# LayerNorm's sums back on VectorE, ties in the order of VectorE's work, and a buffer ring for the second FFN matrix, in a hybrid decoder block on one Trainium2 core

## The chip, the cores and the metric

The kernel runs on one core of a Trainium2 chip. The core has a matrix engine (TensorE, PE in the profile; its weight loads are a row of their own, PEld), a vector engine (VectorE, DVE), a scalar engine (ScalarE, ACT), a general engine (GpSimd, POOL) and a queue engine (SyncE, SP). DMAs are issued from the queues of SP, POOL and ACT. The metric is the device time of one execution in microseconds, as the median of several runs.

## The reference

One layer of a decoder trunk on a sequence of 1024 tokens with a width of 1024, in float32. A token-mixing sub-layer runs a convolution branch and an attention branch side by side and merges them by gates; a SwiGLU sub-layer follows. Cut to what matters:

```python
h = rmsnorm(x, pre_mix_g) * (1 + sc1) + sh1
proj = h @ w_in                                   # conv input, q, k, v, and two gates of 1024 columns
u = u_val * sigmoid(u_gate)
u = causal_depthwise_conv(u, conv_w, conv_b)      # 512 channels, 31 taps
u = silu(layernorm(u, conv_ln_g, conv_ln_b))      # over the 512 channels
y_conv = u @ w_conv_out
y_att = stick_breaking_attention(q, k, v) @ w_att_out
merged = sigmoid(g_conv) * y_conv + sigmoid(g_att) * y_att
x = x + ga1 * rmsnorm(merged @ w_o, post_mix_g)
h = rmsnorm(x, pre_ffn_g) * (1 + sc2) + sh2
gate, up = split(h @ w_ffn_in)                    # 2 x 2816 columns
x = x + ga2 * rmsnorm((silu(gate) * up) @ w_ffn_out, post_ffn_g)
```

`layernorm` takes, for each token, the mean over the 512 channels, subtracts it, and divides by the root of the mean square.

## The kernel before, in words

All activations are held transposed: channels on the 128 partitions, tokens along the free dimension, in two halves of 512 tokens. Float32 products are made from rounded parts: each operand is split into a rounded part ("hi", made by ScalarE) and the remainder ("lo", made by VectorE), and a product is three matmuls (hi hi, hi lo, lo hi) that accumulate in a bank of PSUM. So each operand costs a copy on ScalarE and a subtraction on VectorE.

The gate projections, the FFN's input product and its output product use Winograd's form of the 2 x 2 block product: seven block products instead of eight, for a few additions of weight blocks ("forms" s1 to s4) and of activation blocks (T1 to T4).

The stages in order of time are: the pre-norm and the conditioning vector; projections, convolution and attention; the gate products; the two branch projections and the merge; the product with w_o; the FFN's input product, block by block (`ffn(f)`, 22 blocks); the FFN's output product in four sweeps.

The change touches five places.

1. The gate products and LayerNorm (about 430 to 560 us). `other_five(i)` does, for each of eight pairs of weight tiles, five of the seven block products: T2 into bank ka, T1 into bank kc, T3 onto ka, B22 onto kc, T4 onto ka. Between them VectorE copies the banks out: v = ka + p1 (L814) after T2, w = kc + p1 (L816) after T1. T3 adds onto ka's bank, so it has to wait for v. The forms are s2 (L807), s3 (L809) and s4 (L811) on VectorE. `pair_load(i)` brings the weights (gw*a, gw*b), and s1 with a load and an accumulating DMA from POOL's queue (L795). Each finished piece goes through a sigmoid and out to DRAM from POOL's queue (`sig_out`).

   `ln_all` stands behind the third pair in the program. It loads the four channel tiles of the convolution's output (cr, 128 x 1024 each), and then, for each half of the tokens, makes the sum over the four tiles in `s0_` (the first half of the tile la): one plain load from SP and three accumulating DMAs from POOL (L854), each of which waits for the one before. A matmul with ones (lnm, L856) sums over the partitions. The mean is subtracted from the four tiles (L863), squares are made and added (L865, L867; `s0_` holds one of the squares in between), a second matmul with ones (lnv, L869) sums these, and the reciprocal root, which is put into `s0_` again, multiplies the four tiles (L873). So the second half's sum can enter `s0_` only when the first half has been multiplied.

2. `load_w` loads a tile of weights and splits it (rounding on ScalarE, remainder on VectorE, L153). Behind the merge (L954, L955: y times its gate, and added) the products with w_o begin, one `load_w` for each of eight column blocks.

3. The first blocks of the FFN's input product are written out by hand, in an order that is pinned on TensorE, VectorE and ScalarE. `ffn(0)` and `ffn(1)` are generators, and each `next(...)` emits the next piece of one; `t4(j)` makes T4's block j and its rounding, `lo_of` its remainder (L1228). The second `next(r1)` emits the splits of s2, and a later one those of s1 and s3.

4. `w2_forms(j)` prepares the forms of the FFN's second matrix for the last stage, one call behind each of the blocks f = 10 to 20. It loads four raw blocks (w2r), makes four forms in place (L1118, L1120, L1122, L1124), splits each (L1115) and stores it. Raw blocks come from the ring `wt` of nine buffers, out of which `ffn(f)` takes its s1, s2 and s3 (L1489, L1490, L1497) too. In the same rounds VectorE adds T3's result onto w (L1523), which frees ka's bank for T4.

Everything that isn't pinned is ordered by a planner, which goes through the instructions by priority (the order of the program, moved by offsets), with its own estimates of durations and landing times, and gives each engine and each DMA queue a fixed order. Each engine then runs its order strictly; waits are semaphores between the engines. A tie ("NoSync" dependency) only says in which order two instructions of one engine are to be put; it adds no semaphore.

Of the kernel before, what the change touches and what calls it, by code (L numbers as in the profile page):

```python
# [69 lines left out]
def tile_block(ctx: ExitStack, tc: tile.TileContext, xT, vecs, ada1, ada2, win, wv, wcv, wat, wo, w1, w2, cvw, out):  # L70
# [26 lines left out]
    def load(dst, src):  # L97
        return nc.sync.dma_start(dst, src)
# [648 lines left out]
    with ExitStack() as sG:  # L747
# [32 lines left out]
                load(b, xm_d[k][:, c * CH:(c + 1) * CH])  # L780
            t_ops(j, b11, b12, b21, b22, lambda name: ot(name, F32R))

        pairs, p1s, s1s, t3_done = {}, {}, {}, []

        def pair_load(i):
            wg = wp.tile([P, T], F32, tag="wraw", name=f"gw{i}a")
# [14 lines left out]
        def other_five(i):  # L801
            wg, wu = pairs[i]
            p1 = c21 = p1s[i]
            a11, a12, a21, a22 = wg[:, :CH], wg[:, CH:], wu[:, :CH], wu[:, CH:]
            s1, (s2, s3) = s1s[i], (st(f"g{nm}_{i}") for nm in ("s2", "s3"))
            v, w_ = xt(f"gv_{i}"), xt(f"gw_{i}")
            dve.tensor_tensor(s2, s1, a11, op=ALU.subtract)  # L807
            s2o = w_op(f"s2o_{i}", s2, act, GP)
            dve.tensor_tensor(s3, a11, a21, op=ALU.subtract)  # L809
            s4 = s2  # L810
            dve.tensor_tensor(s4, a12, s2, op=ALU.subtract)  # L811
            ka, kc = bkg(f"ka_{i}"), bkg(f"kc_{i}")
            prod0(ka, s2o, "T2")
            dve.tensor_tensor(v, ka, p1, op=ALU.add)  # L814
            prod0(kc, w_op(f"s1o_{i}", s1, act, GP), "T1")
            dve.tensor_tensor(w_, kc, p1, op=ALU.add)  # L816
            prod0(ka, w_op(f"s3o_{i}", s3, act, GP), "T3", False)
            t3_done.append(nc.cur_bb.bb.instructions[-1].name)
            dve.tensor_tensor(w_, ka, w_, op=ALU.add)
            sig_out(w_, 2 * i + 1, 1)  # L820
            prod0(kc, w_op(f"s4o_{i}", s4, act, dve), "B22", False)
            dve.tensor_tensor(v, kc, v, op=ALU.add)
            sig_out(v, 2 * i, 1)
            prod0(ka, w_op(f"a22_{i}", a22, act, dve), "T4", False)
            dve.tensor_tensor(c21, ka, p1, op=ALU.add)
            sig_out(c21, 2 * i + 1, 0)
# [17 lines left out]
        def ln_all():  # L844
            cr = [hp.tile([P, T], F32, tag="act", name=f"cr{ct}") for ct in range(CONVT)]
            for ct in range(CONVT):
                load(cr[ct], channels(u_d[ct]))
            la, lm = (hp.tile([P, 2, CH], F32, tag="act", name=f"l{nm}") for nm in "am")
            s0_, s1_, mean, sq = la[:, 0], la[:, 1], lm[:, 0], lm[:, 1]
            for c in range(NCH):  # L850
                cs = hs[c]
                load(s0_, channels(u_d[0])[:, cs])
                for ct in (1, 2, 3):
                    nc.gpsimd.dma_start(s0_, channels(u_d[ct])[:, cs], accum_op=ALU.add)  # L854
                pm = psg.tile([P, CH], F32, tag="ln", name=f"lnm{c}", bufs=1)
                mm_ = pe.matmul(pm, ones, s0_, start=True, stop=True)  # L856
                if c == 0:
                    tc.add_manual_dep(mm_.ins, t3_done[0], mybir.DependencyInfo(
                        mybir.DependencyClass.NoSync, mybir.DependencyReason.SCHED_ONLY))
                act.activation(mean, pm, AF.Copy, bias=0.0, scale=1.0 / 512)  # L860
                for ct in range(CONVT):
                    t = cr[ct][:, cs]
                    dve.tensor_tensor(t, t, mean, op=ALU.subtract)  # L863
                    q = (s1_, sq, s0_, sq)[ct]
                    act.activation(q, t, AF.Square)  # L865
                    if ct:
                        dve.tensor_tensor(s1_, s1_, q, op=ALU.add)  # L867
                pvv = psg.tile([P, CH], F32, tag="ln", name=f"lnv{c}", bufs=1)
                pe.matmul(pvv, ones, s1_, start=True, stop=True)  # L869
                rstd_from(s0_, mean, s1_, pvv, 512)  # L870
                for ct in range(CONVT):
                    t = cr[ct][:, cs]
                    dve.tensor_tensor(t, t, s0_, op=ALU.mult)  # L873
            for ct in range(CONVT):
                if ct < 2:
                    back = hp.tile([P, 2, CH], F32R, tag="act", name=f"cb{ct}")
                    back = [back[:, q] for q in range(2)]
                elif ct == 2:
                    back = [sgp.tile([P, CH], F32R, tag="sg", name=f"cb{ct}{q}", bufs=3) for q in range(2)]
                else:  # L880
                    back = pg.tile([P, 2, CH], F32R, tag="cb", name=f"cb{ct}", bufs=1)
                    back = [back[:, q] for q in range(2)]
                chi.append((hhi[HK + ct][:, :CH], back[0]))
                clo.append((hlo[HK + ct][:, :CH], back[1]))
                a, sg, o = cr[ct], flat(la), flat(lm)
                g, b_ = vec[:, C_LNG + ct:C_LNG + ct + 1], vec[:, C_LNB + ct:C_LNB + ct + 1]
                act.activation(sg, a, AF.Sigmoid, bias=b_, scale=g)
                act.activation(a, a, AF.Identity, bias=b_, scale=g)
                ar, sr = (t.rearrange("p (r m) -> p r m", r=PH) for t in (a, sg))
                dve.tensor_tensor(o.rearrange("p (m r) -> p r m", r=PH), ar, sr, op=ALU.mult)  # L890
                for c in range(NCH):
                    act.activation(chi[ct][c], o[:, hs[c]], AF.Copy)
                for c in range(NCH):
                    dve.tensor_tensor(clo[ct][c], o[:, hs[c]], chi[ct][c], op=ALU.subtract)
# [49 lines left out]
        for n in range(KT):  # L944
# [6 lines left out]
            for c in range(NCH):  # L951
                cs = slice(c * CH, (c + 1) * CH)
                load(sg[c], s_d[8 + n][:, cs])
                last = dve.tensor_tensor(sg[c], yb[c], sg[c], op=ALU.mult)  # L954
                dve.tensor_tensor(y[:, cs], y[:, cs], sg[c], op=ALU.add)  # L955
                if n < KT - 1:
                    continue
                if c == 0:
# [35 lines left out]
    with ExitStack() as sF:  # L994
# [80 lines left out]
        load(cb2, cb_d)  # L1075
        for n in range(KT):
            yb = dbank(f"pwo0_{n}")
            w = load_w(wo[n], f"wo0_{n}", act, dve)
            wo_part(yb, w, 0, 0, KT)
            pairs_w[n] = w  # L1080
            if n == HK:
                xr_load(0)
            if n < KT - 1:
                last = evac(0, n, yb)
                for col in ((), (32, 33), (34, 35), (36, 37), (38,), (39,), ())[n]:
                    w = flat2(y2(f"ada2_{col}"))
                    load(w, ada2[col - 2 * KT])
                    with tc.issue_after(last.ins):
                        dot_c(w, cb2, col)
# [15 lines left out]
                              stop=(j == HK - 1 and s == 2), skip_group_check=not first)  # L1105

        def w2_forms(j):
            a11, a12, a21, a22 = (wtmp(f"w2r{q}_{j}") for q in range(4))
            for q, t in enumerate((a11, a12, a21, a22)):
                load(t, w2[j][:, q])  # L1110

# [480 lines left out]
        next(r0)  # L1592
        for j in (2, 3):
            t4(j)
        next(r1)
        for j in (2, 3):
            lo_of("T4", j, h2[HK + j, 0])
        next(r1)
        next(r0)
        next(r0)  # L1600
# [383 lines left out]
```

## Time and profile before

| | us |
|---|---|
| median of 3 runs (lowest, highest) | 1392.19 (1386.76, 1393.64) |
| profiled execution, its own time | 1391.6 |
| its span, first to last instruction | 1389.8 |
| TensorE busy in it | 1370.6 (99%) |
| VectorE busy | 1041.0 (75%) |
| ScalarE busy | 658.5 (47%) |
| GpSimd busy | 122.9 (9%) |

The profile is one execution. "Busy" is the time in which an engine had an instruction running; TensorE's matmuls overlap, so that 512 columns take 0.39 us from start to end and start every 0.23 us. A line such as `L856` is the line of the kernel; where a helper issues the instruction, the line is the helper's, and the names of the tiles (out<-in) tell which call it was. In a list of waits the numbers are the total in us, how often, and the longest. In a timeline they are the start, the duration, the engine, the line, the operation, its tiles and shapes, how many are merged, and in brackets the idle time before and what ended it. In a table of windows each row is a stretch from the span's start, with its length, the busy time of an engine (and its instructions), the granted TensorE clock, the DMA engines' share and the GB/s moved.

### The profile page before, as it was taken

How to read it: one execution, taken by the hardware profiler on the slowest of the kernel's cores; microseconds unless marked ns; L12 is line 12 of the kernel's file. 1: busy time of each engine (PE TensorE's matmuls, PEld its weight loads, DVE VectorE, ACT ScalarE, POOL GpSimd, SP SyncE). 2: the span in 40 equal slices, each digit the busy share in tenths (PEclk: the TensorE clock that was granted, in tenths of full speed). 3: DMA queues.
4: the chain of work that ended last, by engine and by line, in shares of the span. 5: the costliest groups of instructions: out<-in, count | busy, mean ns of one | idle time of the engine just before them, and what ended most of it. 6: DMA issues, size and time to landing. Idle time of an engine off the chain costs nothing.

```text
span 1389.8 us, 18884 instructions
## 1 busy us (share of the span) xinstructions
PE 1370.6 (99%) x6832; PEld 1154.0 (83%) x6832; DVE 1041.0 (75%) x1593; ACT 658.5 (47%) x1169; POOL 122.9 (9%) x268
## 2 busy tenths in 40 slices
PE   8999999999999989999999999999999999999998
PEld 6898888998987868888887888888888888888887
DVE  7997786675877668887597987778787775884354
ACT  6565564464665446413366543324444443433442
POOL 0100001000001221000012200001111110000002
PEclk9999999999999999999999999999999999999999
DMA  9512051141569775865745545456767679596736
GB/s 379 229 41 66 16 167 46 46 137 46 182 222 363 221 209 201 297 222 173 297 137 189 197 144 180 139 194 246 251 224 263 248 257 383 182 346 209 253 114 122
DMA packets 98062, 272.38 MB, mean 196 GB/s; under 512 B 10416, under 2 KB 21808, under 8 KB 96944
## 3 DMA queue, kind: packets, MB, share of 16 engines
q1 hardware_dynamic: 75088, 204.30, 43.4%
q0 software_dynamic: 20160, 61.88, 13.6%
q10 hardware_dynamic: 2720, 4.98, 0.9%
q8 instruction: 54, 0.88, 0.3%
q14 instruction: 40, 0.33, 0.1%
HBM read 199.82 MB, written 71.30 MB: 195 GB/s over the span
## 4 chain that ended last, share of the span: by engine, by line
PE 85%; DMA 7%; DVE 4%; issue 1%; ACT 1%; SPq 0%; ACTq 0%; DVEq 0%; POOLq 0%
PE ka L1104 12%; PE ka L1651 8%; PE kc L1104 7%; PE pwo L1022 6%; PE ke L1213 4%; PE pb L1651 4%; PE pgv L164 3%; PE pya L164 3%; PE pyc L841 3%; PE pv L559 3%; PE ka L459 3%; PE k L459 3%; PE pgg L164 2%; PE pk L164 2%; PE pcv L538 2%; PE pq L164 2%
## 5 line engine op out<-in xcount | busy, mean ns | idle before, releaser
L633 ACT ACTIVATE ka<-z 128x128 f32<-128x128 f32 (+2 forms) x96 | 47.3, 495 | 45.5 <-PE z L632 33.8
L1651 PE MATMUL ka<-gt,w2f 128*128 128x512 f32 x264 | 63.4, 389 | 0.0
L639 DVE TENSOR_TENSOR_SCAN ka<-ka,eye 128x128 f32<-128x128 f32 (+1 forms) x64 | 51.3, 816 | 11.9 <-ACT ka L633 11.7
L644 DVE TENSOR_TENSOR be<-be,ka 128x127 f32<-128x127 f32 (+2 forms) x96 | 53.8, 573 | 6.9 <-ACT be L635 2.0
L1651 PEld LDWEIGHTS ka<-gt,w2f 128*128 128x128 f32 x264 | 49.6, 188 | 10.3
L119 DVE SCALAR_TENSOR_TENSOR ada<-ada,cb 128x1024 f32<-128x1024 f32 x32 | 39.0, 1224 | 18.1 <-DMA ada<-in_ada_dram 17.9
L635 ACT ACTIVATE be<-z 128x127 f32<-128x127 f32 (+2 forms) x96 | 46.9, 496 | 5.4 <-PE tr L658 5.2
L658 PE MATMUL tr<-ident,be 128*128 128x128 f32 x288 | 46.5, 272 | 0.3 <-DVE be L644 0.3
L1213 PE MATMUL ke<-b,w_hi 128*128 128x512 f32 x176 | 44.3, 394 | 0.0
L642 DVE TENSOR_TENSOR_SCAN ka<-ka 128x512 f32<-128x512 f32 x32 | 40.6, 1275 | 3.7 <-ACT ka L633 3.6
L538 PE MATMUL pcv<-ph,cvw 128*128 128x128 f32 x320 | 42.8, 275 | 0.0
L538 PEld LDWEIGHTS pcv<-ph,cvw 128*128 128x128 f32 x320 | 40.3, 191 | 1.0 <-DMA cvw<-in_cvw_dram 0.3
L664 ACT ACTIVATE ahi<-tr 128x512 fp32r<-128x512 f32 x48 | 28.2, 602 | 25.9 <-PE tr L658 17.8
L459 PE MATMUL k<-hhi,a 128*128 128x512 f32 x128 | 40.4, 391 | 0.0
L1213 PEld LDWEIGHTS ke<-b,w_hi 128*128 128x128 f32 x176 | 33.0, 188 | 7.7 <-issue 1.0
L143 ACT ACTIVATE gt<-X 128x512 fp32r<-128x512 f32 x33 | 20.3, 629 | 39.5 <-PE ka L1651 12.5
L665 DVE TENSOR_TENSOR alo<-tr,ahi 128x512 fp32r<-128x512 f32 x48 | 32.1, 685 | 7.8 <-ACT ahi L664 7.5
L658 PEld LDWEIGHTS tr<-ident,be 128*128 128x128 f32 x288 | 34.7, 140 | 3.6 <-PE z L632 0.6
L559 PE MATMUL pv<-wv_hi,hhi 128*128 128x256 f32 x128 | 36.8, 288 | 0.2 <-DVE klo L599 0.2
L559 PE MATMUL pv<-wv_hi,hlo 128*128 128x256 f32 x128 | 36.5, 285 | 0.0
L1637 DVE TENSOR_TENSOR gt<-X,gt 128x512 fp32r<-128x512 f32 x33 | 22.4, 690 | 18.8 <-ACT gt L143 18.7
L559 PE MATMUL pv<-wv_lo,hhi 128*128 128x256 f32 x128 | 36.2, 284 | 0.0
(550 smaller groups left out, 4169.1 us busy)
## 6 DMA issues: line engine op xcount, KB each, us to landing
w_d<-w2o POOLq DMA_DIRECT2D x44, 512.0 KB, 7.6
w2f<-w_d SPq DMA_DIRECT2D x44, 512.0 KB, 4.3
ada<-in_ada_dram SPq DMA_DIRECT2D x32, 512.0 KB, 4.6
w2r<-in_w_dram SPq DMA_DIRECT2D x44, 256.0 KB, 3.8
w1g<-in_w_dram SPq DMA_DIRECT2D x21, 512.0 KB, 3.6
w1u<-in_w_dram SPq DMA_DIRECT2D x21, 512.0 KB, 6.4
cvw<-in_cvw_dram SPq DMA_DIRECT2D x20, 512.0 KB, 3.9
ada_w<-in_ada_dram SPq DMA_DIRECT2D x8, 1024.0 KB, 14.5
```

What stands on the lines that cost most here:

```text
L164: pe.matmul(bank, st[:, cols], mv[k][:, c * CH:(c + 1) * CH], start=(i == 0 and s == 0), stop=(i == n - 1 and s == 2))
L459: pe.matmul(bank_, w[st][:, cols], mvs[mv], start=(first and j == 0 and s == 0), stop=(j == HK - 1 and s == 2), skip_group_check=not first)
L538: pe.matmul(cv[:, gi * TM:(gi + 1) * TM], wts[n][:, at:at + P], ph[:, g, SH - 1 - d:SH - 1 - d + TM], start=(d == 0), stop=(d == SH - 1))
L559: pe.matmul(pv[:, :256], st[k][:, tcols], mv[:, wc], start=(k == 0 and i == 0), stop=(k == KT - 1 and i == 2))
L633: act.activation(kap[:, s_lo:s_hi], z[:, zo:zo + w], AF.Sigmoid, bias=0.0, scale=-0.125)
L639: dve.tensor_tensor_scan(rev, rev, eye[:, CH - w:][:, ::-1], 0.0, op0=ALU.mult, op1=ALU.add)
L644: probs_at[0] = dve.tensor_tensor(beta[:, :m], beta[:, :m], kap[:, s_lo + 1:s_lo + 1 + m], op=ALU.mult).ins.name
L658: pe.transpose(tr[:, o:o + P], probs[ii][:, jo:jo + P], ident)
L1022: pe.matmul(bank_, st[:, cols], mv[k][:, cs], start=(k == 0 and q == 0), stop=(k == KT - 1 and q == 2))
L1104: pe.matmul(bank_, st[:, cols], t[:, mv], start=(first and j == 0 and s == 0), stop=(j == HK - 1 and s == 2), skip_group_check=not first)
L1213: pe.matmul(kbs[f], wes[f][st][:, cols], t[:, mv], start=(i == 0 and j == 0 and st == 0 and mv == 0), stop=(j == HK - 1 and st == 1), skip ...
L1651: pe.matmul(dst, w[st][:, cols], g[mv], start=first and s == 0, stop=last and s == 2, skip_group_check=more)
```

## The change

- LayerNorm's sum over the four channel tiles is made by three additions on VectorE from the tiles cr, for each half, in place of a load and three accumulating DMAs.
- In `other_five(i)` the forms s2 and s3 are ordered on VectorE behind the copy v of the pair before.
- The remainder of w_o's second column block is ordered on VectorE behind the merge's last addition.
- The raw blocks of `w2_forms` get a ring of their own with five buffers; `wt` keeps its nine.
- In the pinned order, the remainders of T4's blocks 2 and 3 come before the second piece of `ffn(1)`.

```diff
-        pairs, p1s, s1s, t3_done = {}, {}, {}, []
+        pairs, p1s, s1s, t3_done, v_done = {}, {}, {}, [], []
...
-            dve.tensor_tensor(s2, s1, a11, op=ALU.subtract)
+            forms = [dve.tensor_tensor(s2, s1, a11, op=ALU.subtract)]
             s2o = w_op(f"s2o_{i}", s2, act, GP)
-            dve.tensor_tensor(s3, a11, a21, op=ALU.subtract)
+            forms.append(dve.tensor_tensor(s3, a11, a21, op=ALU.subtract))
+            if v_done:
+                for f in forms:
+                    tc.add_manual_dep(f.ins, v_done[-1], mybir.DependencyInfo(
+                        mybir.DependencyClass.NoSync, mybir.DependencyReason.SCHED_ONLY))
...
-            dve.tensor_tensor(v, ka, p1, op=ALU.add)
+            v_done.append(dve.tensor_tensor(v, ka, p1, op=ALU.add).ins.name)
...
-                load(s0_, channels(u_d[0])[:, cs])
-                for ct in (1, 2, 3):
-                    nc.gpsimd.dma_start(s0_, channels(u_d[ct])[:, cs], accum_op=ALU.add)
+                dve.tensor_tensor(s0_, cr[0][:, cs], cr[1][:, cs], op=ALU.add)
+                for ct in (2, 3):
+                    dve.tensor_tensor(s0_, s0_, cr[ct][:, cs], op=ALU.add)
...
-                dve.tensor_tensor(y[:, cs], y[:, cs], sg[c], op=ALU.add)
+                merged = dve.tensor_tensor(y[:, cs], y[:, cs], sg[c], op=ALU.add).ins.name
...
+            begin = len(nc.cur_bb.bb.instructions)
             w = load_w(wo[n], f"wo0_{n}", act, dve)
+            if n == 1:
+                for ins in nc.cur_bb.bb.instructions[begin:]:
+                    if ins.engine == mybir.EngineType.DVE:
+                        tc.add_manual_dep(ins, merged, mybir.DependencyInfo(
+                            mybir.DependencyClass.NoSync, mybir.DependencyReason.SCHED_ONLY))
...
-            a11, a12, a21, a22 = (wtmp(f"w2r{q}_{j}") for q in range(4))
+            a11, a12, a21, a22 = (pv.tile([P, CH], F32, tag="w2r", name=f"w2r{q}_{j}", bufs=5) for q in range(4))
...
-        next(r1)
         for j in (2, 3):
             lo_of("T4", j, h2[HK + j, 0])
+        next(r1)
```

## The prediction

> **What bounds the kernel now.** First the page's head, to see which engine has no room.
>
> ```profile
> span 1389.8 us, 18884 instructions
> PE 1370.6 (99%) x6832; PEld 1154.0 (83%) x6832; DVE 1041.0 (75%) x1593; ACT 658.5 (47%) x1169; POOL 122.9 (9%) x268
> ```
>
> TensorE (PE) is busy for all but 19.2 us. VectorE (DVE) has a quarter of the span free. The change leaves TensorE's matmuls as they are, so it can gain only where TensorE stands still or runs at a lower clock. Next, then, TensorE's own waits, longest first.
>
> ```profile
> PE lnm L856 <- DMA la<-u_d: 4.8, 1, 4.8
> ...
> PE ka L459 <- ACT s2o L143: 0.8, 1, 0.8
> PE ka L1104 <- DVE uw L1523: 0.6, 1, 0.6
> ...
> PE lnv L869 <- DVE la L867: 0.4, 1, 0.4
> ...
> PE ka L1104 <- DVE T_2o L1228: 0.3, 1, 0.3
> ```
>
> The largest single wait is one matmul of the LayerNorm mean (lnm) that waits for a DMA into la. All five lie in stages that the change touches. The windows right behind the largest one, with the granted clock in the third column from the right, show that it also costs speed:
>
> ```profile
> 517.00:520.00 3.00, 2.98 (x5) 0.50 0.25 48
> 520.00:523.60 3.60, 3.60 (x11) 0.58 0.28 108
> ```
>
> A matmul's time goes with the clock, so this lost 2.98 x (1 - 0.50) + 3.60 x (1 - 0.58) = 3.0 us. [...] Last, the chain that ended last, at the same place: four transfers one behind the other.
>
> ```profile
> 496.27 2.81 DMA la<-u_d
> 499.62 5.84 DMA la<-u_d
> 505.75 4.37 DMA la<-u_d
> 510.63 6.34 DMA la<-u_d
> ```
>
> The sum of the second column half takes from 496.27 to 510.63 + 6.34 = 516.97, and lnm waits for it. The place costs 4.8 + 3.0 = 7.8 us.
>
> The sum below is made against the profiled execution, 1391.6 us (its span and 1.8 us around it). The median of the runs shown, 1392.19, stands 0.6 above it.
>
> **LayerNorm's sums (main term).** Removed: two loads on SP's queue, six accumulating DMAs on POOL's, and POOL's waits between them, behind which the pairs' own accumulates and the s_d stores stood. Added: six DVE additions of 128x512 in f32. The nearest rows are the subtractions on the same tiles:
>
> ```profile
> 480.34 0.69 DVE L809 TENSOR_TENSOR gs<-gw4a,gw4b 128x512 f32<-128x512 f32 x1 [4.34 <-DMA gw4b<-in_win_dram]
> 480.95 2.49 DVE L863 TENSOR_TENSOR cr<-cr,lm 128x512 f32<-128x512 f32 x4
> ...
> 493.74 2.50 DVE L873 TENSOR_TENSOR cr<-cr,la 128x512 f32<-128x512 f32 x4
> ...
> 509.32 0.69 DVE L446 TENSOR_TENSOR a<-gw5b,a 128x512 fp32r<-128x512 f32 x1
> ```
>
> Four in a row take 2.49, so one step is (2.49 - 0.69)/3 = 0.60 us and six cost 3.6 us of DVE. Can they replace the DMA in time? The second half's sum overwrites the buffer that L873 reads for the first half, so it may start at 493.74 + 2.50 = 496.24. Even put behind everything that DVE had queued before the wait (last row, ends 510.01), three additions end at 510.01 + 2 x 0.60 + 0.69 = 511.9. TensorE ran out of work at 517.0 - 4.8 = 512.2. So the wait goes, and the lower clock with it: 7.8 us. The additions' cover is the pairs' matmuls, which fill TensorE; without that cover the three ahead of one lnm cost 1.9 us. I take 0.6 back for new small waits, the size of the two others in this stage (0.8 and 0.4); the bounds are a gain of 0.4 (the lnv wait goes too) and a loss of 3 (about a half's additions and one round through ScalarE).
>
> **The pair's forms.** s2 and s3 (L807, L809) now stand behind the last pair's copy v (L814).
>
> ```profile
> 442.62 0.69 DVE L807 TENSOR_TENSOR gs<-gs,gw1a 128x512 f32<-128x512 f32 x1 [0.44 <-DMA gw1a<-in_win_dram]
> 443.34 0.69 DVE L814 TENSOR_TENSOR gv<-ka,ga 128x512 f32<-128x512 f32 x1
> ```
> ```profile
> 444.18 2.09 PE L459 MATMUL ka<-T3o,s3o 128*128 128x512 f32 x8 [0.83 <-ACT s2o L143]
> ```
>
> Here s2 of the second pair waits for its weights with v of the first pair behind it. The 0.8 us wait of TensorE ends 0.15 us after v's end (444.03): T3 writes the bank that v must have read. The view puts the wait down to ScalarE's s2o, which ended about then. With the tie v goes first: gain 0.8, at least 0. In turn s2 and s3 queue behind v, and behind s2 wait its rounding on ScalarE, the remainder and the next pair's T2 product. That is three steps of about 0.7 us, against T1, T3, B22 and T4 of the running pair (12 matmuls each) on TensorE. Without this cover each pair pays 2 us. The 4.34 us for gw4b in the fence above it held up LayerNorm's subtractions; under the tie that block is awaited later, behind them or not at all.
>
> **T4's order.** The remainders of two T4 blocks (L1228) move ahead of the split of s2 of block 1.
>
> ```profile
> 813.05 0.69 DVE L1095 TENSOR_TENSOR s2o<-s,s2o 128x512 fp32r<-128x512 f32 x1 [1.22 <-ACT s2o L143]
> 813.66 0.69 DVE L1228 TENSOR_TENSOR T_2o<-y,T_2o 128x512 fp32r<-128x512 f32 x1
> ```
>
> ```profile
> 811.21 0.63 ACT L1224 ACTIVATE T_2o<-y 128x512 fp32r<-128x512 f32 x1 [3.17 <-DVE y L1244]
> ```
>
> DVE idles 1.22 us for s2o's rounding, up to 813.05, while T_2o's remainder stands behind it, whose own rounding was done at 811.84. The new order uses that hole: the 0.3 us wait goes, and s2o, moved one or two steps of 0.6, is used only after T4. Gain 0.3, bounds 0 and 0.3.
>
> **The ring of five for w2r.** The raw blocks leave the ring of nine that they shared with s1, s2, s3.
>
> ```profile
> DVE w2r L1118 <- DMA w2r<-in_w_dram: 29.1, 10, 5.2
> ```
> ```profile
> 1027.57 0.69 DVE L1118 TENSOR_TENSOR w2r<-w2r,w2r 128x512 f32<-128x512 f32 x1 [2.75 <-DMA w2r<-in_w_dram]
> ...
> 1029.63 0.68 DVE L1523 TENSOR_TENSOR uw<-ka,uw 128x512 f32<-128x512 f32 x1
> ```
> ```profile
> 1031.23 0.84 PE L1104 MATMUL ka<-T_0o,a 128*128 128x512 f32 x3
> ```
> ```profile
> 1013.83 0.33 SPq L98 DMA_DIRECT2D w2r<-in_w_dram  x1
> ...
> 1019.24 3.33 SPq L98 DMA_DIRECT2D w2r<-in_w_dram  x3
> ```
>
> DVE waits for these blocks in ten of eleven rounds, with L1523 behind, which frees T4's bank. L1523 ends at 1030.31 and T4 starts at 1031.23, so 0.9 us of slack hides a usual wait; only the longest (5.2) came through, as the 0.6 us above. Now one block of a round loads early and three after the last round's puts. A ring of five, four of them live, allows the same. I take half: gain 0.3, between 0.6 and the loss of the last rival.
>
> **The second w_o block.** Its remainder moves behind the last merge.
>
> ```profile
> 649.16 1.22 DVE L153 TENSOR_TENSOR wo_lo<-wo_raw,wo_hi 128x1024 fp32r<-128x1024 f32 x1
> ```
>
> It stood ahead of the last additions of y. TensorE has no wait there, so I cost it at 0; the first w_o block's 24 matmuls cover it. The bounds are 0 and a loss of 0.4, if the remainder lands behind both last mlo instead.
>
> **Sum.** 7.8 + 0.8 + 0.3 + 0.3 + 0 - 0.6 = 8.6 us; 1391.6 - 8.6 = **1383.0 us**. With every term at its better end 9.9 (1381.7); with each edge at its worse 4.4 (1387.2).
>
> **Rival 1: VectorE blocked ahead of time.** The additions depend only on the cr loads, so the planner can place them in DVE's holes early in the first pair. The tile's answer:
>
> ```profile
> L98 SPq DMA_DIRECT2D cr<-u_d x4: 326/538/714, 430.2 to 433.9; - x4
> ...
> DMA to landing us min/median/max: 7.7/10.3/12.1
> ```
>
> The last cr lands between 433.9 + 10.3 = 444.2 and 433.9 + 12.1 = 446.0. An addition queued ahead of v (443.34) would end 0.7 later and v 0.7 after that, at 445.6 to 447.4, and T3 would start 0.15 behind, while TensorE had been free since 444.18 - 0.83 = 443.35. That is 2.4 to 4.2 us of idle time, with 0 to 3.0 more for the clock, as the wait is nearer to the 0.8 or to the 4.8 above: 1385.4 to 1390.2, and I take 1388. For it speaks that DVE today waited 4.34 us behind a load placed too early; against it, that the additions stand behind three pairs in the program. [...]
>
> **Rival 2: lnm still waits.** The change does not do what it says: the planner moves lnm forward as far as it thinks the sum is done, and DVE runs late by one load of the 4.34 us kind. TensorE then idles 4.3 again and loses 3.0: 1383.0 + 7.3 = 1390.3. Against it stands the 0.4 us wait of lnv, which already goes by DVE's sums.
>
> **Rival 3, slower: the ring of five.** If all late blocks land later by x, T4 waits x - 0.9 in each of ten rounds. With x = 2.5 this eats all gains and 0.5% more; below that it does not decide. The rounds' worst wait exceeds the usual one by 5.2 - 2.75 = 2.45; if all ten were 3.8 later (a wait of 6.5), 10 x 2.9 = 29: 1412 us. Against it: the issue pattern above is already that of five.
>
> **How the numbers follow.** About 0.5% (7.0 us) is what a measurement of this kernel can tell: faster is below 1385.2, slower above 1399.2. Forecast 0.60, with 0.53 of it below 1385.2; rival 1 0.18; rival 2 0.10; rival 3 0.08; the remaining 0.04 is unnamed, 0.01 of it faster, 0.02 same, 0.01 slower. Faster 0.54, same 0.07 + 0.18 + 0.10 + 0.02 = 0.37, slower 0.09. The range goes from 1380 (better ends, and the runs' scatter) to 1392, which takes in rivals 1 and 2.
>
> **What would show it.** The lnm rows have no wait and no window from 430 to 560 has a clock below 1.00; POOL has no line for la; v stands ahead of the next s2; T_2o's wait is gone; w2r's wait on DVE stays near 29 us. Wrong would be a TensorE wait above 1 us in the pairs, or L1523 among TensorE's waits in more than one round.

## The result

The changed kernel takes 1403.64 us (median of six runs, 1402.11 to 1407.53) against 1392.91 for the kernel before beside it: a ratio of 1.009 with a 95% interval of 1.0064 to 1.0116. It is slower by 0.9%. One of the six executions of the kernel before took 2805.31 us; it stands in that median and is left out of the ratio. The profiled execution took 1402.58 us, 11.0 more than that of before.

### The profile page after: what moved, and what is told of

Same layout as the page of the kernel before. It is cut to its first block, busy times and chain, and to the rows that moved or that the text cites. A ratio compares the mean times of both kernels' runs of the same rounds, so it can differ in the third digit from the quotient of the medians.

```text
span 1400.8 us, 18877 instructions
## 1 busy us (share of the span) xinstructions
PE 1375.2 (98%) x6832; PEld 1153.3 (82%) x6832; DVE 1043.1 (74%) x1599; ACT 657.3 (47%) x1169; POOL 117.8 (8%) x262
## 4 chain that ended last, share of the span: by engine, by line
PE 77%; DVE 8%; DMA 8%; issue 4%; ACT 2%; SPq 0%; DVEq 0%; ACTq 0%
PE ka L1661 8%; PE ka L1114 8%; PE pwo L1026 6%; PE kc L1114 5%; DMA w2r<-in_w_dram 4%; PE ke L1223 4%; PE pb L1661 4%; PE ka L459 3%; PE pgv L164 3%; PE pyc L845 3%; PE pya L164 3%; PE pv L559 3%; PE pgg L164 2%; PE pk L164 2%; PE pcv L538 2%
## 5 line engine op out<-in xcount | busy, mean ns | idle before, releaser
L1661 PE MATMUL ka<-gt,w2f 128*128 128x512 f32 x264 | 63.4, 389 | 0.0
L644 DVE TENSOR_TENSOR be<-be,ka 128x127 f32<-128x127 f32 (+2 forms) x96 | 53.7, 573 | 6.9 <-ACT be L635 2.0
L1128 DVE TENSOR_TENSOR w2r<-w2r,w2r 128x512 f32<-128x512 f32 x11 | 7.6, 692 | 47.2 <-DMA w2r<-in_w_dram 47.2
L1538 ACT ACTIVATE uw<-uw 128x512 f32<-128x512 f32 x22 | 13.9, 631 | 59.3 <-DVE uw L1536 59.0
L1114 PE MATMUL ka<-b,a 128*128 128x512 f32 x132 | 36.0, 398 | 1.2 <-DVE a L1105 1.2
```

Source lines behind the costliest of these rows:

```text
L644: probs_at[0] = dve.tensor_tensor(beta[:, :m], beta[:, :m], kap[:, s_lo + 1:s_lo + 1 + m], op=ALU.mult).ins.name
L1114: pe.matmul(bank_, st[:, cols], t[:, mv], start=(first and j == 0 and s == 0), stop=(j == HK - 1 and s == 2), skip_group_check=not first)
L1661: pe.matmul(dst, w[st][:, cols], g[mv], start=first and s == 0, stop=last and s == 2, skip_group_check=more)
```

## The profile after

The page's head of the changed kernel:

```profile
span 1400.8 us, 18877 instructions
PE 1375.2 (98%) x6832; PEld 1153.3 (82%) x6832; DVE 1043.1 (74%) x1599; ACT 657.3 (47%) x1169; POOL 117.8 (8%) x262
```

TensorE is 4.6 us busier with the same 6832 matmuls, and stands still 6.4 us more (25.6 against 19.2). Its waits, longest first (total, how often, longest):

```profile
PE ka L1114 <- DVE uw L1533: 6.6, 7, 1.3
...
PE kc L459 <- ACT s1o L143: 3.4, 1, 3.4
PE ka L1661 <- ACT gb L143: 1.5, 1, 1.5
...
PE ka L1114 <- DVE a L1105: 1.2, 2, 0.6
PE ka L459 <- DVE gv L818: 1.0, 1, 1.0
```

The waits that the change was to remove are gone: lnm, lnv and T_2o are no longer there. In their place stand a wait in seven rounds of the FFN for L1533 (L1523 before), and one of 3.4 us in the pairs for s1o.

LayerNorm did what the first term said. The second half's last addition starts at 488.9 us (before, the last transfer landed at 517.0), the lnm that follows doesn't wait, and in the windows in which the clock was 0.50 and 0.58 before it is full:

```profile
L858 DVE TENSOR_TENSOR la<-la,cr x4: 687/688/693, 445.3 to 488.9; 128x512 f32<-128x512 f32 x4
```
```profile
517.00:520.00 3.00, 3.00 (x15) 1.00 0.43 88
520.00:523.60 3.60, 3.60 (x17) 1.00 0.70 217
...
533.60:537.00 3.40, 3.35 (x8) 0.52 0.39 152
537.00:541.00 4.00, 4.00 (x20) 1.00 0.14 19
...
1195.60:1199.00 3.40, 3.40 (x9) 0.51 0.41 154
1199.00:1203.00 4.00, 4.00 (x19) 0.99 0.39 131
```

But the half clock is back at two other places: behind the wait for s1o (3.35 x 0.48 = 1.6 us lost) and at the start of the first output sweep. In both stretches one matmul of 512 columns starts 0.43 us behind the other, against 0.23 us at full clock.

How the stages moved is read from the first and last start of a few groups of matmuls. Here the product T2 of the FFN, before and after:

```profile
L1104 PE MATMUL ka<-T_0o,s2o x66: 387/389/397, 801.5 to 1148.9; 128*128 128x512 f32 x66
```
```profile
L1114 PE MATMUL ka<-T_0o,s2o x66: 389/389/389, 798.5 to 1156.9; 128*128 128x512 f32 x66
```

The FFN stage went from 347.4 to 358.4 us. The same reading for all stages and all kernels of this study (us; "pairs" is from the first pair's T2 product to the first product with w_o, "FFN" from the first to the last T2 product, "sweep" from the first product of the first output sweep to the first of the second):

| kernel | first pair's T2 | w_o begins | pairs | FFN | sweep |
|---|---|---|---|---|---|
| before | 438.4 | 647.2 | 208.8 | 347.4 | 60.8 |
| after | 438.4 | 644.2 | 205.8 | 358.4 | 64.2 |
| ring undone (e1) | 439.0 | 646.0 | 207.0 | 346.5 | 61.4 |
| ring alone (e2) | 441.7 | 650.0 | 208.3 | 363.1 | 62.0 |
| sums alone (e3) | 438.6 | 640.9 | 202.3 | 348.0 | 64.8 |
| tie alone (e4) | 440.1 | 651.8 | 211.7 | 346.7 | 61.8 |
| ring of seven (e5) | 438.8 | 644.3 | 205.5 | 346.8 | 61.1 |
| ring of six (e6) | 444.1 | 651.8 | 207.7 | 348.3 | 62.5 |
| no ring, no tie (e7) | 445.9 | 645.5 | 199.6 | 346.3 | 63.4 |
| late tail (e8) | 439.5 | 645.9 | 206.4 | 346.5 | 61.5 |
| tie, s1o ahead (e9) | 441.4 | 641.7 | 200.3 | 346.9 | 62.0 |
| sums behind v (e10) | 443.9 | 643.7 | 199.8 | 346.1 | 62.7 |
| the same, ring of seven (e11) | 441.0 | 642.5 | 201.5 | 345.9 | 61.9 |
| e9 once more (e12) | 439.0 | 643.6 | 204.6 | 345.9 | 60.9 |

The column "pairs" differs almost by waits alone: less TensorE's idle time and what it loses at half clock there, the stage is 199.4 to 199.8 us in thirteen of the fourteen profiles, and 200.8 in e4. Where the first pair's T2 starts late by a wait just ahead of it (e2, e4, e6, e7, e9, e10), the wait for v behind it is 0.7 us or less, against 0.8 to 2.5 in the others. So this column favours those six, and a profile can differ by 4 us from another of the same kernel (e9, e12).

So the 11.0 us of the changed kernel are: 3.0 gained in the pairs, 11.0 lost in the FFN, 3.4 lost in the first sweep, and 0.4 gained elsewhere.

**The FFN.** VectorE's wait for the raw blocks, and the times from issue to landing, after and before:

```profile
DVE w2r L1128 <- DMA w2r<-in_w_dram: 47.2, 10, 5.5
```
```profile
DMA to landing us min/median/max: 3.1/5.8/9.5
```
```profile
DMA to landing us min/median/max: 2.9/3.8/7.6
```

The wait was 29.1 us before. One round of the changed kernel, in order of time:

```profile
1042.07 2.49 DVE L1125 TENSOR_TENSOR w2o<-w2r,w2o 128x512 fp32r<-128x512 f32 x4
1042.79 2.65 SPq L98 DMA_DIRECT2D w2r<-in_w_dram  x4
...
1045.99 0.96 SPq L98 DMA_DIRECT2D w1u<-in_w_dram  x1
...
1051.32 0.69 DVE L1128 TENSOR_TENSOR w2r<-w2r,w2r 128x512 f32<-128x512 f32 x1 [5.35 <-DMA w2r<-in_w_dram]
1051.93 0.68 DVE L1533 TENSOR_TENSOR uw<-ka,uw 128x512 f32<-128x512 f32 x1
1052.66 0.53 PEld L1114 LDWEIGHTS ka<-T_0o,a 128*128 128x128 f32 x3 [1.57 <-DVE uw L1533]
```

The four remainders (L1125) are the last reads of the old blocks; each frees a buffer. All four loads, the three that the round still needs and the first of the next round, are issued behind them. In the round of before that the prediction shows, the row "1019.24 3.33 ... x3" merges three issues. Taken apart, only the first stands ahead of the remainders, which began at 1020.92:

```profile
1019.24 0.33 SPq L98 DMA_DIRECT2D w2r<-in_w_dram  x1
```
```profile
1021.64 0.93 SPq L98 DMA_DIRECT2D w2r<-in_w_dram  x2
```

The first is let go by the remainder of a tile of another use of the shared ring (s4o), as the round's first load at 1013.83 is (s3o); the other two, at 1021.64 and 1022.24, wait for the first two remainders of w2r. Call a block late whose load waits for the remainders of the round before: the shared ring of nine has two late blocks in a round, and the ring of five has three. It is so in all ten rounds of both profiles. Late blocks are issued 0.6 us apart but land 2.0 to 2.5 us apart (1025.48 and 1027.48 before; 1046.58, 1048.68 and 1051.22 now), so one more of them makes the form's start later by about one landing. The form's first step began 1027.57 - 1020.92 = 6.65 us behind the first remainder then, and 1051.32 - 1042.07 = 9.25 us now. L1533 stands directly behind it (before, L1523 stood behind three steps of the forms), which takes back some of these 2.6 us, but not all.

**The pairs.** The last pair's s1o on ScalarE, and TensorE's wait for it:

```profile
530.80 0.63 ACT L896 ACTIVATE hhi<-lm 128x512 fp32r<-128x512 f32 x1 [1.11 <-DVE lm L894]
531.34 0.61 ACT L896 ACTIVATE cb<-lm 128x512 fp32r<-128x512 f32 x1
531.86 1.23 ACT L891 ACTIVATE la<-cr,vec 128x1024 f32<-128x1024 f32 x1
532.99 0.61 ACT L143 ACTIVATE s1o<-gs 128x512 fp32r<-128x512 f32 x1
```
```profile
533.65 1.22 PE L459 MATMUL kc<-T1o,s1o 128*128 128x512 f32 x2 [3.42 <-ACT s1o L143]
```

s1o waits for no data here: the last transfer into its tile had landed at 513.4 (started 508.1, 5.3 to landing). It stands in ScalarE's queue behind LayerNorm's swish (L891, L892, L896), and that in turn waits for VectorE's product L894.

## The experiments

Twelve runs were made, of eleven kernels (e12 is e9's). The kernel before beside them had medians of 1391.47 (e1 to e4), 1391.47 (e5 to e8), 1391.43 (e9 to e11) and 1390.4 us (e12); ratios are to these runs.

### e1: the ring undone

The changed kernel with w2r in the shared ring again.

```diff
-            a11, a12, a21, a22 = (pv.tile([P, CH], F32, tag="w2r", name=f"w2r{q}_{j}", bufs=5) for q in range(4))
+            a11, a12, a21, a22 = (wtmp(f"w2r{q}_{j}") for q in range(4))
```

> The changed kernel with the raw blocks w2r put back into the ring of nine that s1, s2, s3 use; all else as changed. Theory ring (the ring of five costs the FFN stage 11 us, because its loads stand behind the last round's puts): the FFN stage is 347 us again as before the change instead of 358, L1533's waits on TensorE fall from 6.6 to about 0.6 us, and the time is 1403.6 - 11 = 1392 if the late start of the first sweep stays, 1389 if that goes too. Theory plan (the loss comes from VectorE's other work and from the shifted order upstream, the ring is innocent): the time stays within 3 us of 1403.6.

1392.26 us, ratio 1.0003 [0.9987, 1.0018]. The FFN is back at 346.5 us and VectorE's wait at 31.2 us. So the ring is all of the loss against before; but the rest of the change, which should have gained 8.3 us, gains nothing. The 3.4 us wait for s1o is still there.

### e2: the ring alone

The kernel before with the ring of five.

> The kernel before with only the ring of five for w2r. Theory ring: the FFN stage grows by about 11 us, w2r's wait on VectorE from 29 to about 47 us, the time is 1392.9 + 11 = 1404, up to 1407 if the first sweep starts late as well. Theory plan: the time stays at 1392.9 within 3 us.

1410.77 us, ratio 1.0127 [1.0098, 1.0157], above what was expected (1404 to 1407).

```profile
PE ka L1104 <- DVE uw L1523: 10.2, 8, 1.5
```
```profile
PEld ka L1104 <- DVE uw L1523: 13.6, 8, 1.9
```

The FFN takes 363.1 us, 15.7 more. The first line understates it: TensorE's matmuls are modelled to end 0.39 us after they start, while they start every 0.23 us, so a part of each pause counts as busy. The weight loads (second line) show 13.6 us. The median is 19.3 us above that of the kernel before, 3.6 more than the FFN accounts for; in the profile a wait of 2.6 us ahead of the first pair adds to it.

### e3: the sums alone

The kernel before with LayerNorm's sums on VectorE.

> The kernel before with only LayerNorm's sums on VectorE (no tie of the forms). Theory tail (the sums remove 7.8 us, but LayerNorm's swish moves up among the last pairs, and ScalarE's queue then holds the last pair's s1o, which costs 3.4 us and 1.7 at half clock): the stage of the pairs ends 2 to 3 us earlier than before, 1390. Theory tie (the tie of the forms makes the new wait, because s1o, s2o, s3o of the last pair come late): without the tie the new wait is gone and the time is 1392.9 - 7.8 = 1385.

1388.78 us, ratio 0.9973 [0.996, 0.9987]. In the pairs 6.5 us are gained (208.8 to 202.3), and a new wait is in it:

```profile
PE ka L459 <- DVE gv L814: 2.0, 1, 2.0
```

There is no wait for s1o, as the theory of the tie had it; the time lies between the two that were expected (1385 and 1390). This profile's first sweep is 4.0 us longer than in that of before, with a wait of 2.1 us and half clock (a granted clock of 0.83 from 1180 to 1190) at its start; e7 to e12 show it at 60.9 to 63.4 us with the same code there, so that it varies from one execution to the next.

### e4: the tie alone

The kernel before with s2 and s3 ordered behind the pair before's v.

> The kernel before with only the tie of s2 and s3 behind the last pair's v; the sums by DMA, the ring, T4's order and the second w_o block as before. Theory tail: lnm still waits for the DMA (4 to 8 us with the clock), the tie alone is worth 0 to 1 us: 1392 to 1393. Theory tie: the last pairs get a wait of 2 to 4 us of their own: 1395 to 1398.

1398.09 us, ratio 1.0046 [1.0029, 1.0062]: the tie alone costs 0.5%. The waits of TensorE, and ScalarE ahead of the last pair's s1o:

```profile
PE lnm L860 <- DMA la<-u_d: 4.3, 1, 4.3
...
PE kc L459 <- ACT s1o L143: 4.1, 3, 2.2
```
```profile
537.05 1.06 ACT L143 ACTIVATE wc_hi<-wc_raw 128x1024 fp32r<-128x1024 f32 x1 [4.96 <-DMA wc_raw<-in_wcv_dram]
...
540.58 0.63 ACT L143 ACTIVATE s1o<-gs 128x512 fp32r<-128x512 f32 x1
```

Here LayerNorm is late as before, and no swish stands there. s1o stands behind the rounding of another weight tile, which waits for its load, and behind LayerNorm's reciprocal root (between the two rows); in the kernel before it stands ahead of both, at 534.41. So a wait for s1o comes with the tie, whatever it is put behind. Of the three waits in the second row one of 1.1 us stands ahead of the first pair (see the last section); the two in the pairs are 0.8 and 2.2 us, less than half of the 6.6 us that the time grew by. Where the rest is lost these profiles don't show.

### e5: a ring of seven

The kernel before with rings of seven for w2r and for the shared ring.

```diff
-            return pv.tile([P, CH], F32, tag="wt", name=name, bufs=9)
+            return pv.tile([P, CH], F32, tag="wt", name=name, bufs=7)
...
-            a11, a12, a21, a22 = (wtmp(f"w2r{q}_{j}") for q in range(4))
+            a11, a12, a21, a22 = (pv.tile([P, CH], F32, tag="w2r", name=f"w2r{q}_{j}", bufs=7) for q in range(4))
```

> The kernel before, with w2r in a ring of its own of seven buffers and the shared ring cut from nine to seven (memory allows fourteen of both). Theory 'late blocks': a ring of five holds one block of the next round and leaves three to be issued only when the last round's puts have freed their buffers; these land too late. A ring of seven holds three of the next round and leaves one, the first of its burst. So VectorE's wait for w2r falls from the 53.7 us that the ring of five alone showed to 30 us or less (29.1 before), TensorE's waits for L1523 fall from 10.2 us in 8 rounds to under 1 us, and the FFN stage is back from 363 us to 346 to 349 us; the time is 1389 to 1394 us against 1391.5. Rival 'a ring of its own': the loss is from the separation itself (the burst of four blocks with w1u behind it, whatever its age), or from fewer buffers for s1, s2, s3: the stage stays above 355 us and the time above 1400 us.

1392.55 us, ratio 1.0006 [0.9993, 1.002].

```profile
DVE w2r L1118 <- DMA w2r<-in_w_dram: 12.3, 10, 1.4
```

No wait for L1523 is left and the FFN takes 346.8 us. One block of a round is late here, the first of its burst. The median landing is 6.3 us, as long as with five (6.2), so it is not the length of the transfers that hurts, but when they may begin. The rival, the separate ring as such, falls.

### e6: a ring of six

As e5 with six for w2r and eight for the shared ring.

> The kernel before, with w2r in a ring of its own of six buffers and the shared ring cut from nine to eight. It leaves two late blocks a round in place of three (ring of five) or one (ring of seven). Theory 'late blocks': the landing of the last late one sets the wait, so TensorE's waits for L1523 lie between those of five (10.2 us) and of seven: 1 to 6 us, VectorE's wait for w2r 30 to 48 us, the FFN stage 349 to 358 us against 347.4 before and 363.1 with five. Rival 'a ring of its own': all as with five.

1400.64 us, in one execution.

```profile
DVE w2r L1118 <- DMA w2r<-in_w_dram: 32.3, 11, 6.0
```
```profile
PE ka L1104 <- DVE uw L1523: 1.5, 1, 1.5
```

The waits lie between those of five and seven, as expected, and the FFN takes 348.3 us, a little under the range. The time does not follow from that. This execution was already 5.7 us late at the first pair's T2 product, by a wait that comes in some executions (see e7). And between the first product with w_o and the FFN it takes 156.7 us, against 154.3 before; e5 takes 156.6 there. Both show a wait of 1.4 us for a norm's sums on VectorE in that stage:

```profile
PE psx L1048 <- DVE xsum L1181: 1.4, 1, 1.4
```

With a ring of its own the first block's forms are made already at 677 to 689 us, among those sums. VectorE's wait for w2r goes 53.7, 32.3, 12.3 us with five, six and seven buffers (three, two and one late block a round), and the shared ring of nine, with two late blocks, has 29.1, near the ring of six: that is the mechanism.

### e7: neither ring nor tie

e1 without the tie of s2 and s3. Left are the sums, T4's order and the tie of w_o.

> The changed kernel with w2r back in the shared ring and without the tie of s2 and s3: LayerNorm's sums on VectorE, T4's order and the tie of the second w_o block are left. If the parts add up, the sums alone (-3.7 us) and what the undone ring leaves unexplained (undone ring +0.4 us, less sums -3.7, less tie +6.4, so -2.3 for T4's order and the w_o tie) give 1391.5 - 6 = 1385.5 us. Theory 'the tie is what is lost': no wait for lnm, none over 1 us for s1o, the product with w_o begins 5 to 7 us earlier than in the kernel before (647.2), and the time is 1384 to 1388 us. Rival 'the tie has nothing to do with it': the 3.4 us wait for s1o at 533 us stays and the time is 1390 to 1394 us, as with the undone ring alone.

1389.16 us, ratio 0.9979 [0.9969, 0.9989], a little over the expected range; the product with w_o begins 1.7 us earlier than in the kernel before, not 5 to 7. The 3.4 us wait at 533 us is gone; the last pair's s1o now stands ahead of the swish:

```profile
532.02 0.62 ACT L143 ACTIVATE s1o<-gs 128x512 fp32r<-128x512 f32 x1
533.98 0.63 ACT L896 ACTIVATE hhi<-lm 128x512 fp32r<-128x512 f32 x1 [1.34 <-DVE lm L894]
```

The pairs take 199.6 us, 7.4 less than with the tie in e1. But this profile has another wait in front of them, in a place that the change doesn't touch:

```profile
439.71 1.22 PE L459 MATMUL kc<-T1o,s1o 128*128 128x512 f32 x2 [3.24 <-ACT s1o L143]
```

With the half clock behind it (a granted clock of 0.95 from 425 to 440 and 0.86 from 440 to 460) the first pair's T2 is 7.5 us late, and no wait for v follows. Against e3, which has neither T4's order nor the w_o tie, the ratios agree (0.9979 and 0.9973): these two edits are too small to show in the time.

### e8: the tail issued later

e1, with LayerNorm's swish issued behind the last pair in the program (`ln_all` made a generator that stops ahead of its last loop).

> The changed kernel with w2r back in the shared ring, with the tie kept, and with LayerNorm's last loop (scale, sigmoid, product) issued only behind the last pair in the program. Theory 'tail': that loop's ScalarE work, now ready some 30 us earlier, stands ahead of the last pair's s1o; put behind the pairs it frees it, the 3.4 us wait for s1o and its half clock go, and the time is 1387 to 1390 us against 1392.3 with the ring undone alone. Theory 'tie': s2 and s3 behind v make each last pair late whatever stands beside them; waits for s1o, s2o or s3o of 3 us in all stay, and the time is 1391 to 1394 us.

1390.62 us, ratio 0.9996 [0.9985, 1.0008].

```profile
535.26 1.13 PE L459 MATMUL kc<-T1o,s1o 128*128 128x512 f32 x2 [3.42 <-ACT s1o L143]
```

The planner put the swish where it had stood, with the third tile's and the fourth's sigmoid still ahead of s1o. So the edit didn't do what it was to do, and this run tells the two theories not apart.

### e9 and e12: s1o ahead of the swish, the tie kept

e1 with one more tie, on ScalarE.

```diff
+            begin = len(nc.cur_bb.bb.instructions)
+            s1o = w_op(f"s1o_{i}", s1, act, GP)
+            s1_act.append([ins.name for ins in nc.cur_bb.bb.instructions[begin:]
+                           if ins.engine == mybir.EngineType.Activation][0])
-            prod0(kc, w_op(f"s1o_{i}", s1, act, GP), "T1")
+            prod0(kc, s1o, "T1")
...
-                act.activation(sg, a, AF.Sigmoid, bias=b_, scale=g)
+                sgm = act.activation(sg, a, AF.Sigmoid, bias=b_, scale=g)
+                if ct >= 2:
+                    tc.add_manual_dep(sgm.ins, s1_act[-1], mybir.DependencyInfo(
+                        mybir.DependencyClass.NoSync, mybir.DependencyReason.SCHED_ONLY))
```

So that the last pair's name is known there, the last loop stands behind the pairs in the program, as in e8.

> The changed kernel with w2r back in the shared ring, the tie kept, and one more tie, on ScalarE: LayerNorm's swish of the third and fourth channel tiles stands behind the rounding s1o of the last pair (it stood ahead of it in the changed kernel). Theory 'place on ScalarE': the tie of s2 and s3 is harmless by itself; it makes the planner put the last pair's s1o behind that swish, and this is what TensorE waits for. Then the 3.4 us wait for s1o and the half clock behind it go, no other wait of over 1 us takes its place between 500 and 560 us, the product with w_o begins 4 to 5 us earlier than with the ring undone alone (646.0), and the time is 1386 to 1390 us. Rival 'late forms': what is late is the pair's forms themselves, which stand on VectorE behind the pair before; the wait moves to the remainder of s1o, to s2o or to v, and stays at 2 us or more: 1390 to 1394 us.

1385.18 us, ratio 0.9954 [0.9938, 0.997], the fastest of the study. ScalarE and TensorE at the place (the sigmoid is L896 in this kernel, L891 in the changed one):

```profile
531.98 0.63 ACT L143 ACTIVATE s1o<-gs 128x512 fp32r<-128x512 f32 x1 [1.97 <-PE ka L459]
532.51 1.23 ACT L896 ACTIVATE la<-cr,vec 128x1024 f32<-128x1024 f32 x1
```
```profile
532.66 0.73 PE L459 MATMUL kc<-T1o,s1o 128*128 128x512 f32 x2 [0.72 <-ACT s1o L143]
```

The wait falls from 3.42 to 0.72 us, no half clock follows (a granted clock of 1.00 from 530 to 560), and the pairs take 200.3 us, as without the tie. It is the place on ScalarE, and the forms being late on VectorE costs nothing that can be seen. Against e8, which differs by this tie alone, the ratio falls from 0.9996 to 0.9954, by 0.4%; against e1, where the last loop stands elsewhere in the program too, by 0.5%.

The same kernel was run again, since it came out faster than the kernels without the tie:

> The kernel with w2r in the shared ring, the tie kept and the last pair's s1o ahead of the swish on ScalarE, once more, with more runs. Its five runs had a ratio of 0.9954 [0.9938, 0.997], against 0.9973 to 0.9979 for four kernels without the tie. If the tie itself is worth something (the prediction had 0.8 us for it), the ratio stays at 0.9954, 1384 to 1386.5 us, with an interval below 0.997. If the lower time was the scatter of few executions (a stall ahead of the first pair comes in some and not in others), it goes to 0.997 to 0.998, 1387.5 to 1389 us.

1385.34 us, ratio 0.996 [0.9944, 0.9976]. The median stays; the interval's upper end, 0.9976, is a little over the bound that was set. The eleven executions of the two runs lie at 1382.7 to 1388.5 us, the 46 of the four kernels without the tie (e3, e7, e10, e11) at 1383.5 to 1392.0. That the tie is worth the 3 us between the medians is not shown: e9 differs from e7 by the place of LayerNorm's last loop and by the tie on ScalarE too, and the profiles show no gain in the pairs (200.3 and 204.6 us against 199.6 in e7 and 202.3 in e3). In e12 against e3 the profile's gain stands in the FFN and the first sweep (2.1 and 3.9 us), where the program is the same but for T4's order. This stays open.

### e10: the sums behind v

e7, with the additions ordered behind the first pair's v.

```diff
+                for f in adds:
+                    tc.add_manual_dep(f.ins, v_done[0], mybir.DependencyInfo(
+                        mybir.DependencyClass.NoSync, mybir.DependencyReason.SCHED_ONLY))
```

> The changed kernel with w2r back in the shared ring, without the tie of s2 and s3, and with one new tie: the three additions of LayerNorm's sum are ordered on VectorE behind the first pair's copy v. In the run with the sums alone TensorE waited 2.0 us for that v, since an addition stood ahead of it and waited for a load. Expected: that wait falls to 0.9 us or less (0.8 before), no wait for lnm, and the time is 1386 to 1389 us (sums alone 1388.8, the same without the two other ties' loss). Rival: the addition's load was not what held v, the wait stays at 1.5 to 2 us, and the time is that of the sums alone, 1388 to 1390.

1388.73 us, ratio 0.9975 [0.9965, 0.9985]. No wait for v in the first pair is left (one of 0.4 us comes later), but the time is that of e7 and e3. In its profile the first pair's T2 is late again (443.9), so the wait might not have been on the path in this execution anyway, and the two theories are not told apart. In e11, which has the same order there, T2 is less late (441.0) and v is awaited for 1.5 us all the same: there VectorE waits ahead of v for s4o's rounding and for weights.

### e11: the same with a ring of seven

> As the kernel with the sums behind v, with w2r in a ring of its own of seven and the shared ring at seven. VectorE's wait for w2r falls from about 27 to about 12 us, but TensorE lost under 1 us there already, so the time is within 1.5 us of the one with the shared ring. Rival: with two buffers fewer s1, s2, s3 come late somewhere once VectorE is ahead; then TensorE shows new waits in the FFN stage and the time is over 2 us longer.

1388.16 us, ratio 0.9974 [0.9961, 0.9987]. VectorE's wait for w2r is 12.3 us against 28.9 in e10, and the time is the same. That wait was hidden already (the FFN takes 345.9 us against 346.1), and between w_o and the FFN 2.8 us are lost as in e5.

## Why the prediction was wrong

Forecast were 1383.0 us; 1403.64 came, outside the range. Rival 3, put at 0.08, is what happened, and one of the gains turned into a loss. Both signs that the prediction had named as wrong came: a wait of TensorE above 1 us in the pairs (3.4), and L1533 among its waits in more than one round (seven).

- **LayerNorm's sums, 7.8 us: right in mechanism and size.** lnm's wait and the half clock behind it went. By themselves the sums shorten the pairs by 6.5 us with a new wait for v of 2.0 us in them (e3), and by 9.2 us where that wait is missing (e7, whose first pair was late already). In the changed kernel the sum in the pairs is 7.8 less 3.4 (s1o) less 1.6 (its half clock), with 0.4 for lnv and -0.2 for v: 3.0, as measured.
- **The tie, "gain 0.8, at least 0": wrong in sign.** Alone it costs 0.5% (e4). The step that failed is the count of cover: "three steps of about 0.7 us, against T1, T3, B22 and T4". It looked at VectorE and at the operations that the tie names. But with s2 and s3 later the planner also put the last pair's s1o, which doesn't read them, later in ScalarE's queue. That it does so with the tie, and not without it, is shown (e1 against e7, e4 against the kernel before); that the reason is its one estimate for all engines is not. e4 shows s1o behind a weight's rounding, e1 behind the swish, and e9, which puts it ahead, has the wait and its half clock back. The gain of 0.8 didn't come either: TensorE waits 1.0 us for v in the changed kernel and 0.9 in e1.
- **The 0.6 us for new small waits: mis-sized.** The wait for s1o and its clock cost 5.0 us, more than the bound of 3; in e1 the same wait costs 6.5, since the half clock lasts twice as long (a granted clock of 0.67 from 530 to 540, so 10 x 0.33 / 0.5 = 6.6 us, against 3.41).
- **The ring of five, "gain 0.3": wrong; it costs the FFN 11.0 us in the changed kernel and 15.7 alone.** Two sentences failed: "A ring of five, four of them live, allows the same", and against rival 3 "the issue pattern above is already that of five". They rest on a reading of the merged row of three loads at 1019.24 as "three after the last round's puts". Only two are: the first began 1.7 us ahead of the remainders that free w2r's own buffers, in a buffer that another use of the shared ring had left. So the ring of nine had two late blocks in a round and not three. Five buffers, four of them live, make it three; a ring of six, with two, gives nearly the waits of before (e6).
- **Rival 3's formula: right place, price too high.** It took T4 to wait x - 0.9 in ten rounds, and to decide from x = 2.5. In the two rounds compared above the form began 2.6 us later, just past that point, which would be 10 x 1.7 = 17 us; 11.0 were lost. L1533, which the rival left where it was, now stands two steps of the forms earlier.
- **T4's order, 0.3: right** as far as it can be seen. The wait for T_2o is gone; in the time e7 against e3 shows nothing. The second w_o block, 0: no wait there.
- **Rival 1 (VectorE blocked ahead of v): there, but small.** The first addition stands ahead of v and waits for its load:

```profile
441.55 0.69 DVE L856 TENSOR_TENSOR la<-cr,cr 128x512 f32<-128x512 f32 x1 [0.62 <-DMA cr<-u_d]
...
443.48 0.69 DVE L818 TENSOR_TENSOR gv<-ka,ga 128x512 f32<-128x512 f32 x1
```

 TensorE waits 1.0 us for v in the changed kernel, 2.0 in e3 and 2.5 in e12 (where VectorE had first waited 3.2 for a weight tile, gw0b), against 2.4 to 4.2 in the working. **Rival 2** (lnm still waits) didn't come.
- **The first sweep, 3.4 us: not foreseen.** It begins with a wait for gb (1.5 us) and a stretch at half clock (0.51 in the window above). The kernels with the shared ring of nine show 60.8 to 64.8 us there, so it is an execution's chance rather than a part of the change.

## What to carry to other kernels

When tiles leave a shared ring for one of their own, don't count buffers alone: look at when each load begins against the reads that free its buffer, because in a shared ring another user's release may be what lets it start. A row that merges several loads hides this; take it apart first. A tie that orders two instructions of one engine can move instructions of other engines that have no part in it; read the new order on every engine around the place, and pin what the critical path needs (here one rounding on ScalarE, worth 0.4 to 0.5%). And a term for "new small waits" ought to include the clock: a wait of 3.4 us cost 5.0 in one profile and 6.5 in another.

## What was not expected of the hardware

- **The lower clock's length.** Behind lnm's wait of 4.8 us in the kernel before, the trace's record of the clock has one stretch at 0.50, of 6.83 us (from 516.16, so that it begins 0.85 us ahead of lnm's matmul). Behind the wait of 3.4 us in the changed kernel the stretch is 3.41 us (from 533.45), and full clock follows (0.52, then 1.00 in the windows above). At the first sweep a stretch of 3.41 us (from 1195.63) follows two gaps of 1.46 and 0.30 us, while none of the seven waits of 0.6 to 1.3 us in the FFN lowered the clock. In e1, too, a wait of 3.4 us has its half clock behind it, but of about 6.6 us (0.67 from 530 to 540). A wait of 2.57 us in e2, ahead of the first pair, lowered nothing (1.00 from 430 to 450), and behind one of 2.1 us in e3, ahead of the first sweep, the row 1180:1190 has 0.83, which is 3.4 us at half clock. So in these profiles the length of a wait alone doesn't tell what it costs at the lower clock; what does is not shown.
- **One wait that comes and goes.** The wait ahead of the first pair (3.24 us in e7's row above) is over 1 us in six of the fourteen profiles (e2, e4, e6, e7, e9, e10) and absent in those of the kernel before and of e5, whose program there is that of e2 and e6. It makes the first pair's T2 1.7 to 7.5 us later than in the kernel before. A single profile's stage total is therefore safer than its span for judging an edit of a few us, and the stage less its waits and half clock safer still.
